# Gate one-hots of four tokens: one VectorE compare for both, multiplications moved to GpSimd, first gathers further apart

## The chip, the cores and the metric

The kernel runs on one core of one Trainium2 chip. The metric is device time in microseconds of one execution, the median of several runs. A profiled execution, recorded by the hardware profiler, goes with them. The engines are TensorE (PE in the profile; its weight loads are PEld), VectorE (DVE), ScalarE (ACT), GpSimd (POOL) and SyncE (SP), which here only issues transfers. Each engine works through its own queue in order.

## The reference

Two layers on a sequence of 256 tokens with 1024 features. Each layer has a part that mixes tokens (convolution, attention, spatial gating), which the change does not touch, and a retrieval part over 128 x 128 = 16384 single-neuron experts:

```
s = einsum('thpk,hpnk->thpn', q, sub_keys)           # 8 heads, two halves, 128 keys each
top_s, top_i = top_k(s, 16)
cand_s = top_s[:, :, 0, :, None] + top_s[:, :, 1, None, :]
cand_i = top_i[:, :, 0, :, None] * 128 + top_i[:, :, 1, None, :]
best_s, best_pos = top_k(cand_s, 16)                 # 16 experts a head, 128 a token
gate = softmax(best_s)
act = gelu(einsum('td,thkd->thk', t, expert_down[experts]))
out = einsum('thk,thkd->td', gate * act, expert_up[experts])
```

## The kernel before

The retrieval part does not gather the experts' weights for most tokens. It multiplies the tokens with all 16384 rows of `expert_down` (128 chunks of 128 experts, a loop over i in `experts`), multiplies the activations by a gate that is zero where a token has not chosen the expert, and then multiplies with all rows of `expert_up` (another 128 chunks, `combine`). A chunk of `down` is a tile of 128 x 1024 f32. SyncE issues its load into `raw`, ScalarE rounds it into `hi` (L246), VectorE takes the rest into `lo` (L239), both tiles with three buffers, and TensorE makes 24 matmuls (L318 to L320: hi x hi, lo x hi, hi x lo for each of eight pieces) of 240 columns. Every second chunk ScalarE applies Gelu to a pair of chunks.

Columns. Of the 256 tokens, 192 (`T`) get their gates in the form of a matrix. The next 48 go through the matmuls, but their 128 activations are fetched later by index (`fetch_act`). The last 16 (`alone`, columns 240 to 255, in both layers: `FT = (240, 240)`) are left out of the matmuls: for these, 16 gathers (`dot_fetch`, GpSimd's indirect DMA, L953) fetch rows of `expert_down` into three buffers, and VectorE forms the dot products (`dot`, L959, 16 of them; each then issues the fetch three further on). `dot_plan` says at which chunk each step is issued: the index is spread over the partitions by DMAs from ScalarE's queue, VectorE adds the layer's offset (`dot_where`, L948), and the first fetch follows.

Gates. The 192 tokens are 48 groups of four. For a token, the chosen experts are 128 pairs (a row key and a column key) and 128 gates. `to_picks` turns them so that the 128 choices lie on the partitions and tokens in the free dimension: `picks` holds one key, `parts` the other and the gate in two f16 parts (a rounded one and the rest). `make_onehots(g)` makes for a group:

- `oh`: the one-hot of the first key, by four GpSimd compares, one a token (L1000, 128 x 128);
- `on`: the one-hot of the second key, by one VectorE compare of 128 x 512 (L1003);
- `og`: two products of `on` with the gate's two parts, by two VectorE multiplications of 128 x 512 (L1005).

`gate_mm(g)` multiplies them on TensorE, two matmuls a token (L1013, L1014), which sums over the 128 choices into a 128 x 128 gate matrix a token in PSUM. `gate_use` (VectorE L1021, ScalarE L1024) then multiplies or stores it into `acts`, and `act_use` (VectorE L1049) multiplies activations that come later. The one-hots have two buffers (`R_ON`), so that group g + 2 is written once `gate_mm(g)` has read. All of this starts in the chunk after the top-k work is done (`start`) and is spread evenly, a group every two chunks, up to chunk 124 (`G_LAST`). In between lie "held" chunks of the next layer's modulation weights (`w_ada`), each one VectorE product with an accumulator (L204): 48 during layer 0's loop, 8 during layer 1's.

The order of the queues in this loop is that of a planner, which takes the program's order, its own costs of instructions and the resulting due times; the splits L246 and L239 have a raised priority. From `combine` on the program's order is kept.

Of the kernel before, what the change touches and what calls it, by code (L numbers as in the profile page):

```python
# [9 lines left out]
F32 = mybir.dt.float32  # L10
F32R = mybir.dt.float32r
F16 = mybir.dt.float16
U32 = mybir.dt.uint32
AF = mybir.ActivationFunctionType
OP = mybir.AluOpType
AX = mybir.AxisListType

P = 128
DEPTH = 2
S = 256  # L20
# [3 lines left out]
GATE_SCALE = 2.0 ** 14  # L24
# [27 lines left out]
SUMS_AT = 7  # L52
NG = T // 4
FT = (240, 240)
DOT_STEP = 25


@with_exitstack
def hybrid_trunk(ctx: ExitStack, tc: tile.TileContext, x_in, c_in, vec_in, w_ada, w_in, w_out, w_pq,
                 keys, down, down_rows, up, rel_bias, sgu_w, sgu_b, out):  # L60
    nc = tc.nc
    consts = ctx.enter_context(tc.tile_pool(name="consts", bufs=1))
# [15 lines left out]
    eps = consts.tile([P, 1], F32, name="eps")  # L78
    nc.vector.memset(eps, EPS)
    spare = consts.tile([P, 1], F32, name="spare")  # L80
    iota = consts.tile([P, P], F16, name="iota")
    nc.gpsimd.iota(iota, pattern=[[1, P]], base=0, channel_multiplier=0,
                   allow_small_or_imprecise_dtypes=True)
    iota2 = consts.tile([P, P, 2], F16, name="iota2")
    nc.gpsimd.iota(iota2, pattern=[[1, P], [0, 2]], base=0, channel_multiplier=0,
                   allow_small_or_imprecise_dtypes=True)
    iota16 = consts.tile([P, 16, 16], F16, name="iota16")
    nc.gpsimd.iota(iota16, pattern=[[1, 16], [0, 16]], base=0, channel_multiplier=0,
                   allow_small_or_imprecise_dtypes=True)
# [4 lines left out]
    flat = arena.rearrange("p a b -> p (a b)")  # L94
    acts = flat[:, :P * T].rearrange("p (i t) -> p i t", t=T)
    hh = consts.tile([P, 2, DC, S], F32R, name="hh")
    picks = consts.tile([P, S], F32, name="picks")
    parts = consts.tile([P, 3, S], F16, name="parts")
    chosen = consts.tile([P, 2, P], F32, name="chosen")
    pairs = consts.tile([P, 2, TS], F32, name="pairs")  # L100
    fold = consts.tile([P, TS], F32, name="fold")
# [185 lines left out]
    for layer in range(DEPTH):  # L287
# [3 lines left out]
        if layer == 0:  # L291
# [5 lines left out]
            n = len(head)  # L297
# [32 lines left out]
    def bank(tag, bufs):  # L330
        return psum.tile([P, 512], F32, name=tag, tag=tag, bufs=bufs)
# [442 lines left out]
    def retrieval(layer, update, late):  # L774
# [80 lines left out]
        def to_picks(b):  # L855
            ps = bank("g", 2)
            for j in range(3):
                nc.tensor.transpose(ps[:, j * P:(j + 1) * P], sel[:, j, :], ident)
            t = slice(b * P, (b + 1) * P)
            if b == 1:  # L860
                nc.vector.scalar_tensor_tensor(chosen[:, 0, :], sel[:, 1, :], float(P), sel[:, 0, :], op0=OP.mult,
                                               op1=OP.add)
                nc.scalar.copy(chosen[:, 1, :], sel[:, 2, :])
                nc.scalar.copy(pairs[TS:], chosen[TS:, :, TS:])
                nc.scalar.dma_start(pairs[:TS], chosen[TS:, :, :TS])
            nc.vector.tensor_copy(picks[:, t], ps[:, 0:P])  # L866
            nc.scalar.copy(parts[:, 0, t], ps[:, P:2 * P])
            g = ps[:, 2 * P:3 * P]
            nc.scalar.activation(parts[:, 1, t], g, AF.Copy, scale=GATE_SCALE)
            nc.vector.scalar_tensor_tensor(parts[:, 2, t], g, GATE_SCALE, parts[:, 1, t],  # L870
                                           op0=OP.mult, op1=OP.subtract)

        def scores(pair):
# [15 lines left out]
        ps = bank("acc", 4)  # L889
# [7 lines left out]
        for pair in range(1, 8):  # L897
            if pair > 1:
                ps = bank("ch", 2)
# [6 lines left out]
        def rest():  # L906
            scores(7)
            for b in range(2):
                for h in range(8):
                    fill.append((0.0, lambda b=b, h=h: expand(b, h)))  # L910
            for b in range(2):
                fill.append((0.7, lambda b=b: cand(b)))
                for h in range(8):
                    fill.append((0.8, lambda h=h: top_cand(h)))
                fill.append((1.6, ranks))
                for j in range(2):
                    fill.append((1.2, lambda j=j: match(j)))
                    fill.append((1.2, lambda b=b, j=j: times(b, j)))
                    fill.append((1.3, lambda j=j: total(j)))
                fill.append((1.0, gate))  # L920
                fill.append((0.5, lambda b=b: to_picks(b)))
        return rest

    def experts(layer, rest):

        onehots = {}
# [25 lines left out]
        def dot_fetch(k):  # L952
            nc.gpsimd.indirect_dma_start(  # L953
                out=R_DOTS[k % 3], out_offset=None, in_=down_rows[:, :],
                in_offset=bass.IndirectOffsetOnAxis(ap=R_DIX[:, 1, k:k + 1].bitcast(U32), axis=0))

        def dot(k):
            row = R_DOTS[k % 3]
            nc.vector.scalar_tensor_tensor(row, row, 1.0, R_DX, op0=OP.mult, op1=OP.mult,  # L959
                                           accum_out=R_DIX[:, 2, k:k + 1])  # L960
            if k + 3 < 16:
                dot_fetch(k + 3)
# [12 lines left out]
        def dot_plan(start):  # L975
            plan = {start: [lambda: nc.scalar.dma_start(dot_ids, chosen[P - alone:, 0, :])],
                    start + 2: [dot_ranks], start + 4: [dot_where]}
            for k in range(3):
                plan[start + 5 + k] = [lambda k=k: dot_fetch(k)]
            for k in range(16):  # L980
                plan.setdefault(start + 9 + k * DOT_STEP // 8, []).append(lambda k=k: dot(k))
            end = start + 9 + 15 * DOT_STEP // 8
            plan[end + 1] = [dot_acts]
            plan[end + 3] = [dot_back]
            assert end + 3 < 108
            return plan
# [4 lines left out]

        def make_onehots(g):
            tile4 = R_ON[g % 2]
            oh = tile4[:, 0].rearrange("p (i n) -> p i n", i=4)
            on = tile4[:, 1].rearrange("p (a n b) -> p a n b", a=2, b=2)
            og = [tile4[:, 2 + j].rearrange("p (a n b) -> p a n b", a=2, b=2) for j in range(2)]
            ts = slice(4 * g, 4 * g + 4)
            for i in range(4):
                t = 4 * g + i
                nc.gpsimd.tensor_scalar(oh[:, i, :], iota, picks[:, t:t + 1], None, op0=OP.is_equal)  # L1000
            wide = lambda j: parts[:, j, ts].rearrange("p (a b) -> p a b", b=2)[:, :, None, :].to_broadcast(
                [P, 2, P, 2])
            nc.vector.tensor_tensor(on, iota2[:, None, :, :].to_broadcast([P, 2, P, 2]), wide(0), op=OP.is_equal)  # L1003
            for j in range(2):
                nc.vector.tensor_tensor(og[j], on, wide(1 + j), op=OP.mult)  # L1005
            onehots[g] = oh, og

        def gate_mm(g):
            oh, og = onehots.pop(g)
            ps = bank("g", 2)  # L1010
            for i in range(4):
                dst = ps[:, i * P:(i + 1) * P]
                nc.tensor.matmul(dst, oh[:, i, :], og[0][:, i // 2, :, i % 2], start=True, stop=False)  # L1013
                nc.tensor.matmul(dst, oh[:, i, :], og[1][:, i // 2, :, i % 2], start=False, stop=True)  # L1014
            return ps

        def gate_use(g, ps, done):
# [194 lines left out]
        start = None  # L1212
        for i in range(128):
            pair, j = divmod(i, 2)
            if j == 0:
                ps = bank("ch", 2)
# [4 lines left out]
            while waiting:  # L1221
                g, gp = waiting.pop(0)
# [6 lines left out]
            if start is None and not fill:  # L1229
                start = i + 1  # L1230
                make_onehots(0)
                make_onehots(1)
                made = 2
                sent = 0
            elif start is not None:
                want = min(NG, -(-NG * (i + 1 - start) // (G_LAST - start)))
                if want < NG and i % 2:
                    want = sent
                while sent < want and len(waiting) < 2:
                    waiting.append((sent, gate_mm(sent)))  # L1240
                    sent += 1
                    if made < NG:
                        make_onehots(made)
                        made += 1
            if alone and start == i + 1:
                dots.update(dot_plan(i + 1))
# [11 lines left out]
        while waiting:  # L1258
            g, gp = waiting.pop(0)
# [13 lines left out]
    for d in range(DC):  # L1273
        update[d]()
        if d in OUT_AT:
            at = max([0] + [n + 1 for n in OUT_AT if n < d])
# [81 lines left out]
```

## Time and profile before

| | before |
|---|---|
| median of 3 runs | 1760.25 us (1757.79 to 1760.39) |
| profiled execution | 1762.3 us |
| its span | 1760.6 us |
| mean granted TensorE clock | 0.988 of full speed |
| busy: TensorE, VectorE, ScalarE, GpSimd | 1698.9, 1474.3, 902.8, 925.3 us |
| four-token groups: GpSimd compares L1000 | 384, 460.4 us, mean 1214 ns |
| VectorE compare L1003, multiplications L1005 | 96 at 442 ns, 192 at 451 ns |
| gathers L953, dots L959 | 32 at 1491 ns, 32 at 1250 ns |

How to read it: the span is the time from the first to the last instruction that the profile has, a little shorter than the execution. Busy time counts instructions in progress, also while one waits for a port or is stretched; a TensorE that is busy is not TensorE at its peak. A line that names a releaser ("<-POOL arena L1000") says what the instruction waited for last. `arena` is one large buffer that holds most tiles, so tiles in it are told apart by line. Rows of a stretch give, for each engine, busy time and in brackets the number of instructions, then the granted clock, the DMA engines' share and GB/s.

### The profile page before, as it was taken

The numbers are of one execution on the slowest core, as the hardware profiler recorded it, in microseconds if no ns is written. First come the engines' busy times: TensorE is split into PE (matmuls) and PEld (weight loads), VectorE is DVE, ScalarE is ACT, GpSimd is POOL, SyncE is SP. The second block draws the span as 40 slices with busy tenths as digits, with TensorE's granted clock in tenths as the row PEclk, the third lists the DMA queues.
The fourth block names the chain that finished last, engine by engine and source line by source line (L and its number), as shares of the span: only waits on it lengthen the run. The fifth ranks groups of instructions, "written<-read, shape, count | busy, mean of one in ns | idle before, by whom it ended". The sixth has DMA issues, their size and how long they took to land.

```text
span 1760.6 us, 32530 instructions
## 1 busy us (share of the span) xinstructions
PE 1698.9 (96%) x11864; PEld 1542.8 (88%) x11864; DVE 1474.3 (84%) x2765; ACT 902.8 (51%) x1475; POOL 925.3 (53%) x729
## 2 busy tenths in 40 slices
PE   7999999889999999999999999998999999999998
PEld 6889999879999978888889899987999998888887
DVE  5858998889989679999976599968778877999996
ACT  2446455335444555555567555543555555555553
POOL 1000204899999388886300011159878857767630
PEclk9999999999999999999999999998999999999999
DMA  9965578989878789999944546778876668999993
GB/s 380 339 226 176 168 212 277 328 262 313 271 244 269 228 272 372 357 398 384 370 148 149 169 148 188 212 229 266 260 207 195 213 201 269 386 382 350 359 372 117
DMA packets 165842, 469.38 MB, mean 267 GB/s; under 512 B 52657, under 2 KB 55121, under 8 KB 164530
## 3 DMA queue, kind: packets, MB, share of 16 engines
q1 hardware_dynamic: 99936, 363.38, 60.5%
q0 software_dynamic: 28544, 96.23, 14.9%
q10 hardware_dynamic: 37202, 7.71, 2.2%
q8 instruction: 93, 1.52, 0.4%
q14 instruction: 67, 0.55, 0.1%
HBM read 457.56 MB, written 9.61 MB: 265 GB/s over the span
## 4 chain that ended last, share of the span: by engine, by line
PE 73%; DVE 11%; issue 5%; POOL 4%; DMA 4%; ACT 1%; ACTq 0%; SPq 0%; POOLq 0%; DVEq 0%
PE acc L1123 32%; PE ch L318 10%; PE ch L319 10%; PE ch L320 10%; DVE lo L239 4%; POOL arena L1000 3%; PE ch L316 3%; DMA arena<-in_down_rows,arena 2%; DMA raw<-in_w_ada 1%; PE ch L399 1%; PE g L1013 1%; PE g L1014 1%; POOL arena L1089 1%; DVE arena L784 1%; DVE arena L782 1%
## 5 line engine op out<-in xcount | busy, mean ns | idle before, releaser
L246 ACT CAST hi<-raw 128x1024 fp32r<-128x1024 f32 x554 | 581.5, 1051 | 610.9 <-PE ch L320 293.8
L239 DVE TENSOR_TENSOR lo<-raw,hi 128x1024 fp32r<-128x1024 f32 x554 | 676.6, 1227 | 123.5 <-ACT hi L246 122.5
L319 PE MATMUL ch<-hh,lo 128*128 128x240 f32 (+1 forms) x2336 | 654.1, 280 | 11.3 <-DVE lo L239 11.0
L318 PE MATMUL ch<-hh,hi 128*128 128x240 f32 (+1 forms) x2336 | 655.7, 282 | 1.4 <-ACT hi L246 1.0
L320 PE MATMUL ch<-hh,hi 128*128 128x240 f32 (+1 forms) x2336 | 649.8, 278 | 0.0
L1000 POOL TENSOR_SCALAR arena<-iota,picks 128x128 f16<-128x128 f16 x384 | 460.4, 1214 | 142.4 <-DVE picks L866 108.4
L319 PEld LDWEIGHTS ch<-hh,lo 128*128 128x128 f32 x2336 | 447.7, 192 | 14.3 <-DVE lo L239 13.7
L318 PEld LDWEIGHTS ch<-hh,hi 128*128 128x128 f32 x2336 | 446.4, 192 | 2.3 <-ACT hi L246 1.2
L320 PEld LDWEIGHTS ch<-hh,hi 128*128 128x128 f32 x2336 | 447.4, 192 | 0.0
L1123 PE MATMUL acc<-hi,hh 128*128 128x512 f32 x1536 | 401.6, 395 | 1.0 <-DVE hh L1064 1.0
L1123 PEld LDWEIGHTS acc<-hi,hh 128*128 128x128 f32 x1536 | 288.3, 188 | 70.8 <-DVE hh L1064 1.8
L1123 PE MATMUL acc<-lo,hh 128*128 128x512 f32 x1024 | 281.8, 395 | 0.0
L1089 POOL DMA_INDIRECT arena<-act_rows,arena x128 | 191.9, 1500 | 87.0 <-PE acc L1123 48.9
L1082 POOL DMA_INDIRECT arena<-in_up,arena x128 | 187.2, 1462 | 87.9 <-DVE arena L1119 62.9
L1123 PEld LDWEIGHTS acc<-lo,hh 128*128 128x128 f32 x1024 | 192.2, 188 | 46.8 <-DVE lo L239 0.7
L1119 DVE SCALAR_TENSOR_TENSOR arena<-arena 128x1024 f32<-128x1024 f32 x126 | 161.6, 1283 | 10.2 <-DMA arena<-in_up,arena 10.2
L204 DVE SCALAR_TENSOR_TENSOR raw<-raw,arena 128x1024 f32<-128x1024 f32 x96 | 117.7, 1231 | 9.9 <-DMA raw<-in_w_ada 6.1
L795 POOL CAST arena<-arena 128x512 f16<-128x512 uint32 x32 | 25.3, 803 | 136.7 <-DVE arena L784 105.5
L1005 DVE TENSOR_TENSOR arena<-arena,parts 128x512 f16<-128x512 f16 x192 | 79.2, 451 | 19.1 <-PE g L1013 19.0
L759 POOL DMA_DIRECT2D arena<-in_keys x2 | 1.1, 563 | 170.4 <-DVE ra L335 117.6
L1013 PE MATMUL g<-arena 128*128 128x128 f16 x384 | 58.5, 224 | 24.4 <-POOL arena L1000 23.2
L1024 ACT ACTIVATE arena<-g 128x344 f32<-128x344 f32 (+23 forms) x96 | 30.9, 324 | 84.9 <-DVE arena L1021 81.7
(243 smaller groups left out, 1719.0 us busy)
## 6 DMA issues: line engine op xcount, KB each, us to landing
raw<-in_down SPq DMA_DIRECT2D x256, 512.0 KB, 4.5
raw<-in_up SPq DMA_DIRECT2D x256, 512.0 KB, 6.3
raw<-in_w_ada SPq DMA_DIRECT2D x96, 512.0 KB, 5.3
raw<-in_w_pq SPq DMA_DIRECT2D x32, 512.0 KB, 3.8
raw<-in_w_in SPq DMA_DIRECT2D x26, 512.0 KB, 4.4
raw<-in_w_out SPq DMA_DIRECT2D x16, 512.0 KB, 4.8
act_rows<-ungated ACTq DMA_DIRECT2D x128, 48.0 KB, 4.2
arena<-in_w_in SPq DMA_DIRECT2D x6, 512.0 KB, 9.8
```

What stands on the lines that cost most here:

```text
L204: op = nc.vector.scalar_tensor_tensor(raw, raw, 1.0, cact, op0=OP.mult, op1=OP.mult, accum_out=mods[layer][:, col:col + 1])
L239: nc.vector.tensor_sub(lo, raw, hi.bitcast(F32))
L246: nc.scalar.copy(hi, raw)
L318: nc.tensor.matmul(dst, hi[:, cols], k[0], start=start, stop=False, **kw)
L319: nc.tensor.matmul(dst, lo[:, cols], k[0], start=False, stop=False, **kw)
L320: nc.tensor.matmul(dst, hi[:, cols], k[1], start=False, stop=stop, **kw)
L1000: nc.gpsimd.tensor_scalar(oh[:, i, :], iota, picks[:, t:t + 1], None, op0=OP.is_equal)
L1005: nc.vector.tensor_tensor(og[j], on, wide(1 + j), op=OP.mult)
L1082: nc.gpsimd.indirect_dma_start(out=R_ROWS[slots[k]], out_offset=None, in_=rows, in_offset=bass.IndirectOffsetOnAxis(ap=where_row[:, k:k + ...
L1089: nc.gpsimd.indirect_dma_start(out=R_ACTS[:, k % (2 * GROUP), :width - T], out_offset=None, in_=act_rows[layer][:, :], in_offset=bass.Indi ...
L1119: nc.vector.scalar_tensor_tensor(R_SUM, v, w8[:, k:k + 1], R_SUM, op0=OP.mult, op1=OP.add)
L1123: nc.tensor.matmul(acc[piece], w, u[:, lo:hi], start=piece not in opened, stop=last, skip_group_check=True)
```

## The change

- `picks` becomes f16 and holds both keys, by group: four tokens' first keys, then their second keys. `parts` keeps the two gate parts alone. `to_picks` writes them with as many copies as before.
- One VectorE compare of 128 x 1024 makes both one-hots of a group, in place of four GpSimd compares and one VectorE compare of half the size. The tile `iota` goes, `iota2` stays.
- The gate is multiplied onto the one-hot of the first key instead of the second, by two GpSimd multiplications of 128 x 512 with two inputs in SBUF, in place of two on VectorE. They read the compare's result.
- `gate_mm` takes the gated one-hot as weights and the bare one as the moving side; its result is the same matrix.
- `dot_plan`: the first three fetches are issued at start + 5, + 8, + 11 instead of + 5, + 6, + 7; dot k at start + 14 + 3k instead of start + 9 + 25k/8 rounded down; the last thus at start + 59 instead of start + 55.

```diff
-    iota = consts.tile([P, P], F16, name="iota")
-    nc.gpsimd.iota(iota, pattern=[[1, P]], base=0, channel_multiplier=0,
-                   allow_small_or_imprecise_dtypes=True)
...
-    picks = consts.tile([P, S], F32, name="picks")
-    parts = consts.tile([P, 3, S], F16, name="parts")
+    picks = consts.tile([P, S // 4, 2, 4], F16, name="picks")
+    parts = consts.tile([P, 2, S], F16, name="parts")
...
-            nc.vector.tensor_copy(picks[:, t], ps[:, 0:P])
-            nc.scalar.copy(parts[:, 0, t], ps[:, P:2 * P])
+            at = picks[:, b * P // 4:(b + 1) * P // 4]
+            nc.vector.tensor_copy(at[:, :, 0, :], ps[:, 0:P].rearrange("p (g t) -> p g t", t=4))
+            nc.scalar.copy(at[:, :, 1, :], ps[:, P:2 * P].rearrange("p (g t) -> p g t", t=4))
...
             for k in range(3):
-                plan[start + 5 + k] = [lambda k=k: dot_fetch(k)]
+                plan[start + 5 + 3 * k] = [lambda k=k: dot_fetch(k)]
             for k in range(16):
-                plan.setdefault(start + 9 + k * DOT_STEP // 8, []).append(lambda k=k: dot(k))
-            end = start + 9 + 15 * DOT_STEP // 8
+                plan[start + 14 + 3 * k] = [lambda k=k: dot(k)]
+            end = start + 14 + 45
...
         def make_onehots(g):
             tile4 = R_ON[g % 2]
-            oh = tile4[:, 0].rearrange("p (i n) -> p i n", i=4)
+            both = tile4[:, 0:2].rearrange("p k (a n b) -> p (k a) n b", a=2, b=2)
+            vals = picks[:, g].rearrange("p k (a b) -> p (k a) b", b=2)
+            nc.vector.tensor_tensor(both, iota2[:, None, :, :].to_broadcast([P, 4, P, 2]),
+                                    vals[:, :, None, :].to_broadcast([P, 4, P, 2]), op=OP.is_equal)
+            oh = tile4[:, 0].rearrange("p (a n b) -> p a b n", a=2, b=2)
             on = tile4[:, 1].rearrange("p (a n b) -> p a n b", a=2, b=2)
-            og = [tile4[:, 2 + j].rearrange("p (a n b) -> p a n b", a=2, b=2) for j in range(2)]
-            ts = slice(4 * g, 4 * g + 4)
-            for i in range(4):
-                t = 4 * g + i
-                nc.gpsimd.tensor_scalar(oh[:, i, :], iota, picks[:, t:t + 1], None, op0=OP.is_equal)
-            wide = lambda j: parts[:, j, ts].rearrange("p (a b) -> p a b", b=2)[:, :, None, :].to_broadcast(
-                [P, 2, P, 2])
-            nc.vector.tensor_tensor(on, iota2[:, None, :, :].to_broadcast([P, 2, P, 2]), wide(0), op=OP.is_equal)
+            og = [tile4[:, 2 + j].rearrange("p (a b n) -> p a b n", a=2, b=2) for j in range(2)]
             for j in range(2):
-                nc.vector.tensor_tensor(og[j], on, wide(1 + j), op=OP.mult)
-            onehots[g] = oh, og
+                gates = parts[:, j, 4 * g:4 * g + 4].rearrange("p (a b) -> p a b", b=2)
+                nc.gpsimd.tensor_tensor(og[j], oh, gates[:, :, :, None].to_broadcast([P, 2, 2, P]), op=OP.mult)
+            onehots[g] = on, og
...
-                nc.tensor.matmul(dst, oh[:, i, :], og[0][:, i // 2, :, i % 2], start=True, stop=False)
-                nc.tensor.matmul(dst, oh[:, i, :], og[1][:, i // 2, :, i % 2], start=False, stop=True)
+                for j in range(2):
+                    nc.tensor.matmul(dst, og[j][:, i // 2, i % 2, :], on[:, i // 2, :, i % 2], start=j == 0,
+                                     stop=j == 1)
```

More of the change, by code (lines that the diff above doesn't have):

```diff
@@ L54 @@
 FT = (240, 240)
-DOT_STEP = 25
 @with_exitstack
@@ L865, in to_picks @@
                 nc.scalar.dma_start(pairs[:TS], chosen[TS:, :, :TS])
-            nc.vector.tensor_copy(picks[:, t], ps[:, 0:P])
-            nc.scalar.copy(parts[:, 0, t], ps[:, P:2 * P])
+            at = picks[:, b * P // 4:(b + 1) * P // 4]
+            nc.vector.tensor_copy(at[:, :, 0, :], ps[:, 0:P].rearrange("p (g t) -> p g t", t=4))
+            nc.scalar.copy(at[:, :, 1, :], ps[:, P:2 * P].rearrange("p (g t) -> p g t", t=4))
             g = ps[:, 2 * P:3 * P]
-            nc.scalar.activation(parts[:, 1, t], g, AF.Copy, scale=GATE_SCALE)
-            nc.vector.scalar_tensor_tensor(parts[:, 2, t], g, GATE_SCALE, parts[:, 1, t],
+            nc.scalar.activation(parts[:, 0, t], g, AF.Copy, scale=GATE_SCALE)
+            nc.vector.scalar_tensor_tensor(parts[:, 1, t], g, GATE_SCALE, parts[:, 0, t],
                                            op0=OP.mult, op1=OP.subtract)
@@ L993, in make_onehots @@
             tile4 = R_ON[g % 2]
-            oh = tile4[:, 0].rearrange("p (i n) -> p i n", i=4)
-            on = tile4[:, 1].rearrange("p (a n b) -> p a n b", a=2, b=2)
-            og = [tile4[:, 2 + j].rearrange("p (a n b) -> p a n b", a=2, b=2) for j in range(2)]
-            ts = slice(4 * g, 4 * g + 4)
-            for i in range(4):
-                t = 4 * g + i
-                nc.gpsimd.tensor_scalar(oh[:, i, :], iota, picks[:, t:t + 1], None, op0=OP.is_equal)
-            wide = lambda j: parts[:, j, ts].rearrange("p (a b) -> p a b", b=2)[:, :, None, :].to_broadcast(
-                [P, 2, P, 2])
-            nc.vector.tensor_tensor(on, iota2[:, None, :, :].to_broadcast([P, 2, P, 2]), wide(0), op=OP.is_equal)
+            both = tile4[:, 0:2].rearrange("p k (a n b) -> p (k a) n b", a=2, b=2)
[3 more added lines that the diff above has]
+            oh = tile4[:, 0].rearrange("p (a n b) -> p a b n", a=2, b=2)
+            on = tile4[:, 1].rearrange("p (a n b) -> p a n b", a=2, b=2)
+            og = [tile4[:, 2 + j].rearrange("p (a b n) -> p a b n", a=2, b=2) for j in range(2)]
             for j in range(2):
-                nc.vector.tensor_tensor(og[j], on, wide(1 + j), op=OP.mult)
-            onehots[g] = oh, og
+                gates = parts[:, j, 4 * g:4 * g + 4].rearrange("p (a b) -> p a b", b=2)
+                nc.gpsimd.tensor_tensor(og[j], oh, gates[:, :, :, None].to_broadcast([P, 2, 2, P]), op=OP.mult)
+            onehots[g] = on, og
         def gate_mm(g):
-            oh, og = onehots.pop(g)
+            on, og = onehots.pop(g)
             ps = bank("g", 2)
```

## The prediction

> **What bounds the kernel now.** I read the engine shares first (TensorE 96%, VectorE 84%: two candidates), then busy time by stretch for the two stages with gates, then the waits inside them, then single instructions.
>
> ```profile
> PE 1698.9 (96%) x11864; PEld 1542.8 (88%) x11864; DVE 1474.3 (84%) x2765; ACT 902.8 (51%) x1475; POOL 925.3 (53%) x729
> ```
> ```profile
> core 0: us, PE busy (x) PEld busy (x) DVE busy (x) ACT busy (x) POOL busy (x), PEclk, DMA share, GB/s
> 240.00:260.00 20.00, 20.00 (x181) 20.00 (x180) 19.97 (x56) 9.51 (x14) 0.00 (x0) 1.00 0.73 215
> 340.00:420.00 80.00, 67.63 (x590) 64.43 (x590) 67.90 (x120) 31.73 (x66) 77.38 (x66) 0.95 0.84 275
> 284.00:582.00 298.00, 276.48 (x2509) 270.43 (x2508) 261.87 (x450) 133.75 (x268) 268.05 (x206) 0.97 0.85 279
> 1150.00:1240.00 90.00, 78.32 (x667) 75.65 (x666) 63.06 (x106) 36.72 (x69) 63.85 (x51) 0.92 0.77 255
> 1240.00:1440.00 200.00, 200.00 (x1921) 198.82 (x1920) 159.06 (x269) 101.63 (x210) 162.80 (x156) 1.00 0.70 215
> 1150.00:1440.00 290.00, 278.32 (x2585) 274.46 (x2584) 222.13 (x374) 138.35 (x277) 226.65 (x206) 0.98 0.72 227
> ```
>
> 284:582 and 1150:1440 are the gating stages of the two layers. The same stretches for VectorE's split (L239, one per chunk), and then for its compare (L1003, one per group of four tokens), count the work:
>
> ```profile
> 340.00:420.00 80.00, 23.91 (x20) 0.95 0.84 275
> 284.00:582.00 298.00, 109.76 (x90) 0.97 0.85 279
> 1150.00:1240.00 90.00, 30.73 (x25) 0.92 0.77 255
> 1150.00:1440.00 290.00, 114.13 (x93) 0.98 0.72 227
> ```
> ```profile
> 340.00:420.00 80.00, 5.45 (x13) 0.95 0.84 275
> 284.00:582.00 298.00, 20.19 (x46) 0.97 0.85 279
> 1150.00:1240.00 90.00, 3.61 (x8) 0.92 0.77 255
> 1150.00:1440.00 290.00, 18.82 (x44) 0.98 0.72 227
> ```
>
> TensorE's floor: 181 matmuls in 20 us without gating are 0.11 us each, so a chunk of 24 takes 2.65 us. Eight gate matmuls at 0.06 us from start to start (rows below) add 0.47 us a group.
>
> ```profile
> 451.18 0.22 PE L1013 MATMUL g<-arena 128*128 128x128 f16 x1
> 451.24 0.22 PE L1014 MATMUL g<-arena 128*128 128x128 f16 x1
> ```
>
> Layer 0 then needs 90 x 2.65 + 46 x 0.47 = 260 us and takes 298: 38 lost. Layer 1 needs 93 x 2.65 + 44 x 0.47 = 267 and takes 290: 23 lost. Most of it lies early: 340:420 has 20 chunks and 13 groups, 59 us of work in 80; 1150:1240 has 25 and 8, 70 in 90. 1240:1440 runs without a gap. What TensorE waits for there (waits of layer 0's stretch; then GpSimd's row of instructions in layer 1, and the landing time of a gather):
>
> ```profile
> PEld L1013 <- POOL arena L1000: 20.4, 22, 2.2
> POOL arena L953 <- DVE arena L948: 14.9, 1, 14.9
> DVE arena L959 <- DMA arena<-in_down_rows,arena: 13.6, 7, 5.2
> ```
> ```profile
> 1139.42 16.83 POOL L1000 TENSOR_SCALAR arena<-iota,picks 128x128 f16<-128x128 f16 x12 [53.91 <-DVE picks L866]
> 1167.47 1.77 POOL L953 DMA_INDIRECT arena<-in_down_rows,arena  x1 [11.22 <-DVE arena L948]
> ...
> 1194.85 1.68 POOL L953 DMA_INDIRECT arena<-in_down_rows,arena  x1 [1.90 <-DVE arena L959]
> 1196.57 6.61 POOL L1000 TENSOR_SCALAR arena<-iota,picks 128x128 f16<-128x128 f16 x4
> ```
> ```profile
> arena<-in_down_rows,arena POOLq DMA_INDIRECT x32, 6.8
> ```
>
> GpSimd's queue is in order. It stands still for 15 and 11 us behind the first gather's index (L948), then goes round fetch, landing, dot, fetch (ten fetches from 1167 to 1196 us) with one-hots queued behind, and the gate matmuls are late. In layer 0 it is also full afterwards (268 of 298 us).
>
> **The change, part by part.**
>
> ```profile
> L1000 POOL TENSOR_SCALAR arena<-iota,picks 128x128 f16<-128x128 f16 x384 | 460.4, 1214 | 142.4 <-DVE picks L866 108.4 <-PE g L1014 33.1
> L1003 DVE TENSOR_TENSOR arena<-iota,parts 128x512 f16<-128x512 f16 x96 | 41.6, 442 | 0.0
> L1005 DVE TENSOR_TENSOR arena<-arena,parts 128x512 f16<-128x512 f16 x192 | 79.2, 451 | 19.1 <-PE g L1013 19.0
> L843 DVE TENSOR_TENSOR arena<-arena 128x1024 f16<-128x1024 f16 x8 | 5.4, 678 | 0.0
> L472 POOL TENSOR_SCALAR_AFFINE_SELECT arena<-arena 128x512 f32<-128x512 f32 x2 | 3.1, 1537 | 17.7 <-DMA arena<-in_sgu_w 17.7
> ```
>
> VectorE, by group: 0.442 + 2 x 0.451 go, one compare of 1024 f16 comes, at L843's 0.678. Instructions overlap the next by 0.08 us (L239 below: 1.21 long, 1.13 to the next start), so two fewer give back 0.16: 0.67 - 0.16 = 0.51 us saved.
>
> GpSimd, by group: four compares go (4 x 1.214 = 4.86 us), two multiplications of 128x512 with two inputs come. No row shows one. What the 1.214 is made of matters more, and GpSimd's CAST of 512 elements (L795) shows it:
>
> ```profile
> 170.03 1.73 POOL L795 CAST arena<-arena 128x512 f16<-128x512 uint32 x1 [7.38 <-DVE arena L784]
> 170.07 1.21 DVE L239 TENSOR_TENSOR lo<-raw,hi 128x1024 fp32r<-128x1024 f32 x1
> ...
> 216.37 0.61 POOL L795 CAST arena<-arena 128x512 f16<-128x512 uint32 x1 [4.14 <-DVE arena L784]
> 216.66 1.40 DVE L239 TENSOR_TENSOR lo<-raw,hi 128x1024 fp32r<-128x1024 f32 x1
> ```
>
> With a two-input VectorE instruction beginning 0.04 us later, the CAST took 1.73 instead of 0.61: it waited for L239's end (171.28) and took 0.48 more. Where it was 0.29 ahead, it kept its 0.61 and L239 grew from 1.21 to 1.40. So the two exclude each other, both ways, and a GpSimd read of 512 elements holds VectorE off until 216.66 + 0.19, 0.48 us after its start. Call what a multiplication holds h. It reads two operands of 512: h lies between 0.48 (both read together) and 1.4 (L472's 1.537, less the 0.13 by which the CAST outlasts its hold). I take 0.9, two reads one after the other, nearest to the CAST, which has the same width and 16-bit output. A multiplication is then 1.05 us alone and about 1.65 with half a VectorE instruction of 1.2 waited out; a group 3.3 instead of 4.86, 70 us less by layer, and GpSimd is no longer full.
>
> The Trainium skill (GPSIMD Engine Reference, 3.1 Elementwise) says that a two-input operation there needs about 2.6 cycles an element, because both operands share one read port; at its 1.2 GHz that is an estimate of 1.11 us for 512. By it h is 1.1, and the sum is rival A's. No row here has a two-input GpSimd operation to hold against it; the CAST's 0.48 for one operand is below half of it.
>
> The price falls on VectorE: each hold pushes it back by h - 0.1 (the overlap), in nine cases of ten (L1021 reads PSUM and one SBUF operand): 2 x 0.9 x 0.8 = 1.44 us a group, less about 0.15 that the short compares cost now (L1003 0.50 below against 0.41). Net 1.44 - 0.15 - 0.51 = +0.78. One period of layer 0, a group and two chunks:
>
> ```profile
> 451.55 0.87 DVE L1005 TENSOR_TENSOR arena<-arena,parts 128x512 f16<-128x512 f16 x2 [0.54 <-PE g L1013]
> ...
> 452.75 1.21 DVE L239 TENSOR_TENSOR lo<-raw,hi 128x1024 fp32r<-128x1024 f32 x1
> 453.88 1.21 DVE L204 SCALAR_TENSOR_TENSOR raw<-raw,arena 128x1024 f32<-128x1024 f32 x1
> ...
> 455.02 0.50 DVE L1003 TENSOR_TENSOR arena<-iota,parts 128x512 f16<-128x512 f16 x1
> ...
> 457.45 0.82 DVE L1005 TENSOR_TENSOR arena<-arena,parts 128x512 f16<-128x512 f16 x2 [0.53 <-PE g L1013]
> ```
>
> The period is 5.90 us, 0.53 of it idle: VectorE works 5.37, after the change 6.15. TensorE needs 2 x 2.65 + 0.47 = 5.77. So layer 0 becomes VectorE's. A dot (L959, of L204's shape, so 1.21) every three chunks adds 0.8 a period over 45 chunks. Layer 0: 45 x 6.15 + 22.5 x 0.8 = 295 us. Layer 1 has eight of L204's products instead of 48 (the group 5 of w_ada alone); without their 1.14 VectorE needs 5.0 a period, 5.8 with dots: TensorE's pace, 46.5 x 5.8 = 270.
>
> Gathers: the first three are 3 chunks apart, the first dot comes 9 chunks after its fetch (24 us or more) instead of 4, against a landing of 6.8. The 13.6 us that VectorE waits go; every later dot keeps about 9 chunks, the last comes some 4 later, at start + 59 of 128. In GpSimd's queue one-hots can now lie between the fetches. The index is ready no sooner, and two groups made ahead cover 11.5 of the 15 and 11 us. For this and for what order the planner gives the queues, which I don't see, I leave 5 us lost in layer 0 and 8 in layer 1.
>
> At nothing: as many gate matmuls and weight loads; the compare waits for the gate matmuls of two groups before, as L1005 does now, with L1021 and L239 behind it (the 0.53 stays, or is the time in which a multiplication reads); gates come after both engines in turn, 0.68 + 3.3 us, inside two periods. If that cover went, some 4 us would show once a layer. The four copies of the picks and the lost iota are under 1 us.
>
> Sum: layer 0 300 against 298 (+2), layer 1 278 against 290 (-12): -10 on the profiled execution's 1762.3 us (span 1760.6). It lies 2 us over the runs' median of 1760.25, so the median goes to about 1750.
>
> **Rivals.** A, slower: the multiplications hold longer and VectorE sets both stages. At h = 1.1, between my 0.9 and L472's 1.4, a period is 6.51 and layer 0 takes 45 x 6.51 + 18 + 5 = 316 (+18), layer 1 24 x 5.8 + 22.5 x 6.2 + 8 = 287 (-3): 1775. At 1.4, some 1810. It decides from h of about 1.0, only 0.1 above my value. For it: VectorE's 262 of 298 us. Against: the short hold of the CAST.
>
> B, faster: both operands are read together, h = 0.5. VectorE needs 5.4 a period, TensorE sets layer 0 too: 22.5 x 5.8 + 22.5 x 6.2 + 5 = 275 (-23), layer 1 -12: 1725. Against: the CAST alone takes 0.48 for one operand.
>
> C, no change: the fetches stay queued ahead of the one-hots, and the early stalls (21 and 20 us) come again. Layer 1 then loses 20 instead of 8: 1762. For it: the 15 and 11 us come from the index, which is not moved.
>
> **How the numbers follow.** The forecast has 0.40 (own range 1740 to 1757), A 0.32, B 0.13, C 0.15. 0.2%, 3.5 us, is about what can be told from no change. Faster: forecast and B, 0.53; same 0.12, slower 0.35 (A, and C's upper part). The range cuts B at its edge and A above h of 1.2: 1726 to 1783.
>
> **What would show it.** GpSimd's multiplication row at 1.5 to 1.9 us mean and about 1.05 at its shortest; the compare near 0.68; L239's mean in layer 0 well above 1.23; VectorE busy over 95% in 284:582's counterpart; no row of L959 waiting for a gather above 1 us; L1013's wait for GpSimd near nothing. I am wrong if L239 isn't stretched (then B), or if TensorE's waits turn to L239 in layer 1 as well (A).

## The result and the profile after

The changed kernel takes 1779.78 us (median of 4 runs, 1779.61 to 1780.29) against 1760.32 for the kernel before (median of 4): a ratio of 1.0113, 95% interval 1.0096 to 1.0131. It is slower by 19.5 us; 1750 was forecast, and the time is near that of rival A, 1775. Layer by layer it is near A too (+18 and -3). From the first to the last pair of chunks (ScalarE's Gelu into `ungated`, one a pair), in profiled executions:

| | layer 0 | layer 1 |
|---|---|---|
| before | 402.6 us | 386.7 us |
| changed | 423.2 (+20.6) | 384.7 (-2.0) |
| forecast | +2 | -12 |

The first part of the profile's page, and busy time by stretch in layer 0 (282:602 is its stage with gates, 344:420 the place where most is lost) and in layer 1:

```profile
PE 1703.7 (96%) x11864; PEld 1548.0 (87%) x11864; DVE 1547.6 (87%) x2573; ACT 901.2 (51%) x1475; POOL 759.3 (43%) x536
```
```profile
282.00:602.00 320.00, 286.00 (x2530) 276.24 (x2530) 302.75 (x356) 133.97 (x270) 164.25 (x112) 0.97 0.80 260
344.00:420.00 76.00, 59.21 (x487) 55.51 (x485) 76.00 (x85) 26.59 (x56) 45.69 (x36) 0.93 0.74 243
1240.00:1440.00 200.00, 199.83 (x1904) 198.61 (x1904) 183.39 (x197) 100.10 (x205) 122.22 (x83) 0.99 0.70 214
```

GpSimd is relieved (268 of 298 us before, 164 of 320 now), with 192 VectorE instructions fewer VectorE is busy for 73 us longer, and in 344:420 it never rests. The groups in layer 0's stage (line, engine, operation, count, busy us, mean ns):

```profile
L235 DVE TENSOR_TENSOR lo<-raw,hi 128x1024 fp32r<-128x1024 f32 x90 | 147.5, 1651 | 7.2 <-ACT hi L242 7.1
L200 DVE SCALAR_TENSOR_TENSOR raw<-raw,arena 128x1024 f32<-128x1024 f32 x44 | 68.6, 1559 | 0.0
L993 DVE TENSOR_TENSOR arena<-iota,picks 128x1024 f16<-128x1024 f16 x46 | 33.7, 733 | 2.4 <-PE g L1009 2.4
```

L235 is the split that was L239: 90 of them took 109.8 us before and take 147.5 now. One group at close range, VectorE first, then GpSimd:

```profile
522.98 0.68 DVE L993 TENSOR_TENSOR arena<-iota,picks 128x1024 f16<-128x1024 f16 x1
523.59 0.54 DVE L1017 SCALAR_TENSOR_TENSOR arena<-arena,g 128x384 f32<-128x384 f32 x1
524.05 1.81 DVE L235 TENSOR_TENSOR lo<-raw,hi 128x1024 fp32r<-128x1024 f32 x1
525.79 2.06 DVE L200 SCALAR_TENSOR_TENSOR raw<-raw,arena 128x1024 f32<-128x1024 f32 x1
527.78 0.08 DVE L200 DVE_READ_ACCUMULATOR raw<-raw,arena 128x1 f32 x1
527.78 1.22 DVE L235 TENSOR_TENSOR lo<-raw,hi 128x1024 fp32r<-128x1024 f32 x1
```
```profile
523.74 3.02 POOL L1000 TENSOR_TENSOR arena<-arena,parts 128x512 f16<-128x512 f16 x2 [2.10 <-DVE arena L993]
```
```profile
L1000 POOL TENSOR_TENSOR arena<-arena,parts x92: 1039/1063/2095, 283.0 to 600.1; 128x512 f16<-128x512 f16 x92
```

The first multiplication begins beside L1017, which reads PSUM, and the next split takes 1.81 us instead of 1.22. The second waits for that split's end, and L200, next in the queue, takes 2.06 instead of 1.21. The third instruction is its old self. A multiplication that waits for nothing takes 1.04 us (the row of L1000's shortest, median and longest, in ns).

Of the signs that the prediction named, the row of multiplications came (mean 1.50 us, shortest 1.04), and so did the stretched split. The compare is a little longer than 0.68 (0.73), VectorE is busy 94.6% of the stage instead of over 95%. The two signs of a better order did not come: TensorE's weight loads for the gates still wait 7.7 us for GpSimd (20.4 before), and one dot still waits 5.9 us for its gather:

```profile
PEld L1009 <- POOL arena L1000: 7.7, 8, 1.6
DVE arena L956 <- DMA arena<-in_down_rows,arena: 5.9, 1, 5.9
```

### The profile page after: what moved, and what is told of

Its sections match the earlier page's. It is cut to its first block, busy times and chain, and to the rows that moved or that the text cites. A ratio compares the mean times of both kernels' runs of the same rounds, so it can differ in the third digit from the quotient of the medians.

```text
span 1777.9 us, 31927 instructions
## 1 busy us (share of the span) xinstructions
PE 1703.7 (96%) x11864; PEld 1548.0 (87%) x11864; DVE 1547.6 (87%) x2573; ACT 901.2 (51%) x1475; POOL 759.3 (43%) x536
## 4 chain that ended last, share of the span: by engine, by line
PE 64%; DVE 16%; issue 9%; POOL 7%; DMA 3%; ACT 1%; SPq 0%; ACTq 0%; DVEq 0%; POOLq 0%
PE acc L1119 33%; POOL arena L1000 6%; PE ch L315 6%; PE ch L314 6%; PE ch L316 6%; DVE lo L235 6%; PE ch L312 3%; PE g L1009 1%; DVE raw L200 1%; PE ch L395 1%; DMA raw<-in_w_ada 1%; DVE arena L780 1%; DMA arena<-in_down_rows,arena 1%; DVE arena L778 1%; PE acc L314 1%
## 5 line engine op out<-in xcount | busy, mean ns | idle before, releaser
L235 DVE TENSOR_TENSOR lo<-raw,hi 128x1024 fp32r<-128x1024 f32 x554 | 758.6, 1379 | 100.4 <-ACT hi L242 98.8
L1000 POOL TENSOR_TENSOR arena<-arena,parts 128x512 f16<-128x512 f16 x192 | 283.9, 1502 | 288.7 <-DVE arena L993 288.4
L1078 POOL DMA_INDIRECT arena<-in_up,arena x128 | 203.6, 1591 | 86.5 <-DVE arena L1115 52.7
L200 DVE SCALAR_TENSOR_TENSOR raw<-raw,arena 128x1024 f32<-128x1024 f32 x96 | 133.2, 1392 | 9.4 <-DMA raw<-in_w_ada 5.9
L950 POOL DMA_INDIRECT arena<-in_down_rows,arena x32 | 46.3, 1447 | 92.1 <-DVE arena L956 49.2
L993 DVE TENSOR_TENSOR arena<-iota,picks 128x1024 f16<-128x1024 f16 x96 | 71.6, 748 | 7.6 <-PE g L1009 7.5
```

Of the source, the lines that this page charges most:

```text
L200: op = nc.vector.scalar_tensor_tensor(raw, raw, 1.0, cact, op0=OP.mult, op1=OP.mult, accum_out=mods[layer][:, col:col + 1])
L235: nc.vector.tensor_sub(lo, raw, hi.bitcast(F32))
L993: nc.vector.tensor_tensor(both, iota2[:, None, :, :].to_broadcast([P, 4, P, 2]), vals[:, :, None, :].to_broadcast([P, 4, P, 2]), op=OP.is_ ...
L1000: nc.gpsimd.tensor_tensor(og[j], oh, gates[:, :, :, None].to_broadcast([P, 2, 2, P]), op=OP.mult)
L1078: nc.gpsimd.indirect_dma_start(out=R_ROWS[slots[k]], out_offset=None, in_=rows, in_offset=bass.IndirectOffsetOnAxis(ap=where_row[:, k:k + ...
```

## The experiments

All times are medians of 4 to 10 runs; ratios are to the kernel before, which ran beside them at 1758.0 to 1759.6 us.

**Both multiplications on VectorE.** Two theories: P, the loss is the port (the name used here for what the CAST and the split of the prediction keep each other from), which GpSimd's two-input multiplications hold against VectorE; Q, the order of the queues and the longer way over two engines.

```diff
-            og = [tile4[:, 2 + j].rearrange("p (a b n) -> p a b n", a=2, b=2) for j in range(2)]
+            og = [tile4[:, 2 + j].rearrange("p (a n b) -> p a b n" if j in (0, 1) else "p (a b n) -> p a b n", a=2, b=2)
+                  for j in range(2)]
...
-                nc.gpsimd.tensor_tensor(og[j], oh, gates[:, :, :, None].to_broadcast([P, 2, 2, P]), op=OP.mult)
+                if j in (0, 1):
+                    nc.vector.tensor_tensor(og[j].rearrange("p a b n -> p a n b"), oh.rearrange("p a b n -> p a n b"),
+                                            gates[:, :, None, :].to_broadcast([P, 2, P, 2]), op=OP.mult)
...
```

> The changed kernel with both multiplications back on VectorE (128x512 f16, two inputs, some 0.45 us each), so that GpSimd makes no gate instruction at all. Theory P (port): GpSimd's two-input multiplications hold VectorE off, 0.85 us each, and that is the loss. Then the split's mean in the gate stages falls back to 1.22 us, a group costs VectorE 0.68 + 0.90 us with no holds, layer 0 goes at TensorE's pace in its second half, and the time is 1735 to 1755 us. Theory Q (order): the loss comes from the order of the queues at the start of the gates, with gathers and dots bunched before the one-hots, and from the longer way of the one-hots over two engines; the bunching stays here, so the time stays at 1765 to 1780.

1732.85 us, ratio 0.9852 (0.9824 to 0.9881): 2 us below P's range, 32 below Q's, and faster than both kernels. VectorE has two more instructions a group and is still quicker through the stage than in the changed kernel (over the whole kernel, the split and then the multiplications):

```profile
L235 DVE TENSOR_TENSOR lo<-raw,hi 128x1024 fp32r<-128x1024 f32 x554 | 675.5, 1223 | 118.9 <-ACT hi L242 114.5 <-PE acc L1124 2.1 <-issue 1.0
L1002 DVE TENSOR_TENSOR arena<-arena,parts 128x512 f16<-128x512 f16 x192 | 71.7, 418 | 0.0
```

**GpSimd writes and reads nothing.**

```diff
-                nc.gpsimd.tensor_tensor(og[j], oh, gates[:, :, :, None].to_broadcast([P, 2, 2, P]), op=OP.mult)
+                for k in range(2):
+                    nc.gpsimd.memset(og[j][:, k], 0.0)
```

> The changed kernel with each GpSimd multiplication replaced by two memsets of the same tile (128x256 each): GpSimd writes as much and waits for the same gate matmuls, but reads nothing. The gates are left out of the result (they are all zero). P: no hold without a read; split back to 1.22 us, VectorE has only the one compare of 0.68 a group, 1725 to 1745 us. A port that is held by writes too, or Q: split still stretched or early stalls as they are, 1765 to 1785.

1723.23 us, 0.9802 (0.9772 to 0.9832), just below P's range; 384 memsets in the same queue, and the split undisturbed:

```profile
L235 DVE TENSOR_TENSOR lo<-raw,hi 128x1024 fp32r<-128x1024 f32 x554 | 675.7, 1224 | 161.1 <-ACT hi L242 155.3 <-issue 2.6 <-PE acc L1120 2.1
L1001 POOL MEMSET arena<- 128x256 f16 x384 | 103.4, 314 | 416.2 <-PE g L1010 306.3 <-DVE arena L817 77.3 <-DVE arena L827 15.0
```

The memsets also need no compare and are shorter, so the time alone does not separate the read from those two. The single instructions do: in layer 0's gate stage 29 of the splits and of L200's products overlap a memset, and they take 1.22 us on average and 1.25 at most. It is the read that holds VectorE off.

**A third multiplication that nobody waits for.**

```diff
+    waste = consts.tile([P, 2, 2, P], F16, name="waste")
...
+            nc.gpsimd.tensor_tensor(waste, oh, gates[:, :, :, None].to_broadcast([P, 2, 2, P]), op=OP.mult)
```

> The changed kernel with a third GpSimd multiplication a group into a tile that nobody reads: not on any chain, and GpSimd has room (164 of 320 us busy in layer 0's gate stage). P: one more hold of 0.85 us a group on VectorE, which has no room in layer 0: 35 to 40 us more there and 5 to 20 in layer 1, 1815 to 1840 us. Q: nobody waits for it, 1778 to 1790.

1846.98 us, 1.0505 (1.0475 to 1.0535), above P's range: 67 us more than the changed kernel, 38 in layer 0 and 30 in layer 1. Work off every chain costs that much, which Q cannot give. Layer 0 fits one hold a group; layer 1 lost more than the 5 to 20 I wrote, because VectorE, busy 183 of 200 us there in the changed kernel (1240:1440), is now full in that layer too (199 of 200 us in 1300:1500).

**One multiplication on each engine.** As the first edit, for j = 1 alone.

> The changed kernel with one of the two multiplications on VectorE (0.42 us) and one left on GpSimd. By the port theory (each GpSimd multiplication holds VectorE off for about 0.85 us) the time lies midway between the changed kernel (1780) and the one with both on VectorE (1733): 1748 to 1762. If the second hold alone were the cost (the first mostly lands beside the PSUM-reading L1017): 1733 to 1745; if a single GpSimd step in the chain costs as much as two: 1768 to 1780.

1745.24 us, 0.9921 (0.9895 to 0.9947), between the two but nearer to VectorE's: a little under the range that I gave for the port theory, and at the upper end of the one for the second hold alone (1733 to 1745). The one multiplication left is mostly one that begins beside the PSUM-reading instruction (some 30 of 46 in layer 0's stage with gates), and the split's mean over the kernel is 1.30 us against 1.38 and 1.22:

```profile
L235 DVE TENSOR_TENSOR lo<-raw,hi 128x1024 fp32r<-128x1024 f32 x554 | 717.2, 1300 | 100.4 <-ACT hi L242 98.6
```

The first hold costs about a quarter of the 47 us between the two kernels, the second the rest: a dose, not a proportional one. This fits the instructions: the first hold pushes VectorE by about 0.6 us and the second by 0.85 (the group at close range above), and each spares it a multiplication of 0.42, a net price of 0.18 and 0.43 us a group.

**The plan of gathers alone.** The changed kernel with the old plan, and the kernel before with the new one:

```diff
             for k in range(3):
-                plan[start + 5 + 3 * k] = [lambda k=k: dot_fetch(k)]
+                plan[start + 5 + k] = [lambda k=k: dot_fetch(k)]
             for k in range(16):
-                plan[start + 14 + 3 * k] = [lambda k=k: dot(k)]
+                plan.setdefault(start + 9 + k * 25 // 8, []).append(lambda k=k: dot(k))
-            end = start + 14 + 45
+            end = start + 9 + 15 * 25 // 8
```

> The changed kernel with the gathers and dots planned as before (fetches at start + 5, 6, 7, dots from start + 9 every 25/8 chunks). The queue that the planner makes of it on GpSimd is nearly the same as the changed kernel's (six multiplications, then six fetches in a row). If the spread is undone by the planner: 1775 to 1785, no change. If the spread helped and only the gates cost: 1790 or more. If the spread hurt: 1770 or less.

> The kernel before with the changed kernel's plan of gathers and dots alone (fetches at start + 5, 8, 11, dots from start + 14 every three chunks). If the planner sorts the queues by its own due times, little moves: 1755 to 1765. If the spread is worth what the prediction took it for (the 13.6 us that VectorE waits for gathers in layer 0, more in layer 1): 1735 to 1750.

1778.3 us (1.0119, 1.0088 to 1.0150) and 1759.75 (1.0007, 0.9989 to 1.0026): neither differs from its own kernel. The profile of the changed kernel shows why. GpSimd's gathers in layer 0 are issued at three-chunk steps in the program, and stand in the queue like this:

```profile
308.12 1.85 POOL L950 DMA_INDIRECT arena<-in_down_rows,arena  x1 [22.09 <-DVE mod L210]
310.28 1.90 POOL L950 DMA_INDIRECT arena<-in_down_rows,arena  x1 [0.30 <-issue]
312.48 0.94 POOL L950 DMA_INDIRECT arena<-in_down_rows,arena  x1 [0.30 <-issue]
318.92 1.68 POOL L950 DMA_INDIRECT arena<-in_down_rows,arena  x1 [5.50 <-DVE arena L956]
321.64 1.68 POOL L950 DMA_INDIRECT arena<-in_down_rows,arena  x1 [1.04 <-DVE arena L956]
325.07 1.68 POOL L950 DMA_INDIRECT arena<-in_down_rows,arena  x1 [1.75 <-DVE arena L956]
326.76 2.05 POOL L1000 TENSOR_TENSOR arena<-arena,parts 128x512 f16<-128x512 f16 x2
```

The first three are 2 us apart, not three chunks, and six precede the fourth group's multiplications. With the old plan the changed kernel's queue has the same order here, its first three fetches at 309.04, 311.17 and 313.37 us. The planner sorts by its own due times, and the edit to the plan is no edit to the queue.

**Gathers and dots pinned.** Each is tied behind what the program issued before it on its engine, so that the written spread holds:

```diff
-            nc.gpsimd.indirect_dma_start(
+            op = nc.gpsimd.indirect_dma_start(
...
+            tc.keep_in_program_order(op)
...
-            nc.vector.scalar_tensor_tensor(row, row, 1.0, R_DX, op0=OP.mult, op1=OP.mult,
-                                           accum_out=R_DIX[:, 2, k:k + 1])
+            tc.keep_in_program_order(nc.vector.scalar_tensor_tensor(
+                row, row, 1.0, R_DX, op0=OP.mult, op1=OP.mult, accum_out=R_DIX[:, 2, k:k + 1]))
```

In the changed kernel:

> The changed kernel with each gather and each dot pinned behind what the program has issued before it on its engine, so that the planner can't pull them forward: in GpSimd's queue five groups' multiplications then come before the first gather and one to three groups between gathers, and dots lie three chunks apart. Theory S (spread): the prediction's gain failed because the planner undid the spread and bunched gathers and dots into the first 30 chunks; pinned, layer 0's chunks 40 to 72 take 115 to 125 instead of 136 us, 1755 to 1768 in all. Theory W (work): VectorE has 303 us of work in 320 in layer 0's gate stage, so a spread only moves it: 1772 to 1785.

In the kernel with both multiplications on VectorE:

> Both multiplications on VectorE, and gathers and dots pinned as above. S: the early stall of both layers goes, 1715 to 1726. W: 1728 to 1738, as without the pin, since TensorE sets most of the gate stage there.

In the kernel before, with the new plan:

> The kernel before (its gates: four GpSimd compares a group, two multiplications on VectorE) with the changed kernel's plan of gathers and dots, pinned in program order as above. With the changed kernel pinned (1760 us) it prices the gates alone at a spread that holds. If the holds are the gates' price and the bunching is a cost of its own in both kernels: 1735 to 1745, some 20 us under the pinned changed kernel. If GpSimd's 268 of 298 us sets layer 0 whatever the order (the prediction's reading of the kernel before): 1752 to 1762, as before.

| gates | planner's order | pinned | layer 0, layer 1 pinned |
|---|---|---|---|
| four GpSimd compares (before) | 1759.2 us | 1758.29, ratio 1.000 (0.9989 to 1.0010) | 403.6, 381.8 us |
| two GpSimd multiplications (changed) | 1779.78 | 1760.41, ratio 1.0013 (0.9998 to 1.0028) | 408.3, 379.4 |
| both multiplications on VectorE | 1732.85 | 1725.11, ratio 0.9808 (0.9782 to 0.9833) | 385.7, 368.1 |

The pin takes 19.4 us from the changed kernel (17.6 by the two ratios, since the runs of the kernel before that stood beside them differ by 2 us), 7.7 from VectorE's, nothing from the kernel before. The changed kernel's chunks 40 to 72 take 108 us pinned (312:420) against 136 (312:448), where theory S had 115 to 125. Layer 0 from chunk 40 to chunk 120 shows each bound: the changed kernel, the changed one pinned, the kernel before pinned, VectorE's pinned.

```profile
312.00:606.00 294.00, 260.97 (x2313) 251.40 (x2312) 282.40 (x326) 120.50 (x250) 157.74 (x109) 0.97 0.79 257
```
```profile
312.00:591.00 279.00, 253.98 (x2313) 245.34 (x2311) 274.09 (x328) 119.46 (x250) 181.88 (x110) 0.99 0.82 272
```
```profile
310.00:586.00 276.00, 252.82 (x2305) 246.38 (x2304) 239.77 (x413) 120.25 (x251) 258.40 (x200) 0.97 0.83 276
```
```profile
310.00:567.00 257.00, 246.17 (x2292) 243.14 (x2291) 241.97 (x420) 121.60 (x252) 30.03 (x20) 0.98 0.87 295
```

In the kernel before GpSimd works 258 of 276 us, and the better order gains nothing. In the changed one pinned VectorE works 274 of 279. In VectorE's, GpSimd works 30, VectorE 242 and TensorE 246 of 257 us.

## Why the prediction was wrong, point by point

- **GpSimd's and VectorE's exclusion: right.** The CAST row told it, and the runs without (both on VectorE, memsets), with less (one each) and with more (a third) bear it out. The Trainium skill (SBUF — State Buffer, Who interferes with whom) has the same rule: a VectorE instruction with two SBUF inputs contends with a GpSimd instruction that reads SBUF, not with one that only writes. The run with memsets agrees (split 1224 ns).
- **The size of a hold: right.** I took 1.05 us for a multiplication alone and pushes of 0.8; measured 1.04, and 0.85 where VectorE pays in full (L200, 2.06 against 1.21), about 0.6 where the multiplication begins beside L1017. That is 1.44 us a group, as forecast. VectorE's work a group was put at +0.78, 75 us for 96 groups; the profile's page has 1547.6 against 1474.3, +73. A came about in time, but not by its condition: with the 0.1 of overlap h is about 0.95, below the 1.0 from which A was to hold, so its nearness to the measured time is luck. The upper bound of 1.4 came from a row that was itself stretched: L472's two instances took 1.38 and 1.70 us, and in the changed kernel one of them takes 0.63. The Trainium skill's rule that spoke against the change (GPSIMD Engine Reference, 3.1 Elementwise, 2.6 cycles an element, an estimate of 1.11 us) is 7% over the shortest row, 1.04 us.
- **The step that failed first: "in GpSimd's queue one-hots can now lie between the fetches".** Between the first six they do not: the planner bunched gathers, dots and the groups behind them into layer 0's chunks 40 to 72, where VectorE, now the bound, could not take them (76.00 of 76 us in 344:420). This is the condition of rival C, which priced it at 12 us, all in layer 1; the loss came in layer 0. I counted the dots over 45 chunks and left 5 and 8 us for the order. Made true by the pin, the step gives 1760.4: 19.4 of the 29.8 us between forecast and measurement. That is still above the forecast's own range (1740 to 1757) and, at a ratio of 1.0013, no gain over the kernel before.
- **The term that was mis-sized: a group every two chunks.** My sum spread 45 groups evenly over 90 chunks. The period that I read at 451 us was an even one, but in the pinned kernel the ten chunks before 312 us have no compare at all and the 80 chunks from chunk 40 on have all 45, 1.125 a period:

```profile
312.00:591.00 279.00, 34.61 (x45) 0.99 0.82 272
```
```profile
312.00:591.00 279.00, 133.23 (x80) 0.99 0.82 272
```

  A group costs VectorE 0.61 + 0.46 + 1.44 us (compare and L1017 from start to start in the rows above, holds), so an eighth more is 0.31 a period and 12 us in 40. My sum for these chunks, 40 x 6.15 + 16 x 1.21 = 265 us, becomes 278; the pinned kernel takes 279. The ten chunks without a group cost less than I had, 28 us at TensorE's pace, so the 90 chunks together take 307 us against the 300 of the forecast, in which 5 were for an order that the pin mends.
- **The waits for gathers: half right.** The 13.6 us that VectorE waited in layer 0 became 5.9. They were not a cost of their own: in the kernel before with the pin no dot waits for a gather in that stage, and it is no faster.
- **Reading GpSimd as layer 0's bound: right in the main.** The kernel before gains nothing by the pin. With both multiplications on VectorE, VectorE works as long in the 80 chunks as in the kernel before (242 and 241 us), GpSimd 28 us instead of 256, and they take 258 instead of 273. What I did not see is that a compare took 1.21 us on average but 0.59 at its shortest, so about half of GpSimd's time in them was not the compare itself. That it was waiting for the port was not shown. Relieving GpSimd was worth what the forecast hoped only if the work did not go to the engine next in line through the port.
- **Layer 1:** forecast -12, changed -2, pinned -7 (and -5 in the kernel before pinned), by single profiled executions. The early stall went with the pin: in 1150:1240 TensorE is busy 87.7 us, 78.3 before. But in 1240:1440, where I had TensorE's pace and where it had no gap before, it is busy 193.7 of 200 us with VectorE at 194.5, and in the stage it waits 7.9 us for the split, 3.7 before: the sign that I gave for A. The kernel before pinned has 193.2 there too, with waits for GpSimd instead, so how much of the missing 5 us is the holds stays open.

## What to carry to other kernels

An instruction moved to an idle engine is not free where the two engines hold each other off: price what it holds, in instructions of the busy engine, before counting what it relieves; here two 0.45 us multiplications taken from VectorE cost it 1.4 us a group. Keeping them, and taking only the compares from GpSimd, was the half of the change that paid (1733 us, pinned 1725, against 1759). And where a planner orders the queues, a new place in the program is a wish: look in the queue whether it was granted, and pin what has to hold.

## What the hardware showed that I had not expected

Four multiplications that were ready together kept the port for their whole length. VectorE's split did not get in between them and took 4.90 us, 3.7 more than alone, while in the usual case above it ran between two:

```profile
1232.77 4.90 DVE L235 TENSOR_TENSOR lo<-raw,hi 128x1024 fp32r<-128x1024 f32 x1
```
```profile
1232.55 4.03 POOL L1000 TENSOR_TENSOR arena<-arena,parts 128x512 f16<-128x512 f16 x4
```

What decides which of the two gets the port at a handover stays open.
